# A roll along the columns of an 8192 x 8192 array: which rows of four each DMA queue takes, and how the last 256 rows are cut

## The chip, the cores and the metric

The kernel runs on one core of a Trainium2 chip. A core has sixteen DMA engines, which move data between the chip's memory (HBM) and itself or the core's on-chip memory (SBUF). Transfers are started by instruction queues: here SP (SyncE), ACT (ScalarE) and POOL (GpSimd). The metric is the device time of one execution in microseconds; lower is better.

## The reference

The input is a float32 array of 8192 rows and 8192 columns (32 KB a row, 268 MB in all), and every row is rotated to the right by 100 columns.

```python
def setup_inputs():
    return {"x": np.random.randn(8192, 8192).astype(np.float32), "shift": 100}

def reference(x, shift):
    return np.roll(x, shift, axis=1)
```

Nothing is computed. Each output row is two runs of its input row: columns 100 and up take the input's columns 0 to 8091, and columns 0 to 99 take its last 100.

## The kernel before

The kernel splits the output's columns at `a`. The shift `s` is 100, `a` is 128 rounded up and then raised by 128 to 256, and `g = a - s` is 156. Columns 256 to 8191 (31,744 bytes a row, 97% of the data) go straight from the input in HBM to the output in HBM; columns 0 to 255 go through SBUF.

**The straight copies (lines 34 to 43).** Rows are seen as blocks of 64: block `c`, then `e` from 0 to 15, then `j` from 0 to 3, so row = 64 c + 4 e + j. There are 128 blocks. One DMA of line 43 copies, for one `c` and one `j`, the sixteen rows `e = 0..15`; these rows lie 128 KB apart, and each of the sixteen DMA engines takes one of them. An engine so works on four neighbouring rows in each block, one for each `j`. The queue is `engines[j % 2]`: rows 0 and 2 of the four are issued by SP and rows 1 and 3 by ACT, in the order j = 0, 1, 2, 3. For the last four blocks (256 rows) each copy is cut into two at column `mid` = 4224, two pieces of 3968 columns (15,872 bytes a row), both on the queue of that `j`. This makes 248 whole and 32 / 2 = 16 half copies on each queue.

Each copy signals a semaphore when it has landed on all its engines. The framework hands out eight semaphores for the copies of SP and ACT in turn, and an instruction that takes one up again waits until the copy before it on that semaphore has landed. So at most four copies of each queue are in flight.

**The strip of 256 columns (lines 60 to 82).** The rows are treated in four groups of 2048. For three rows of every four, POOL loads columns -100 to 155 of the row as one run into a tile `t` (line 73; the first 100 of these are the end of the row before). For the fourth row and for the first row's right part it loads the pieces directly into a second tile `h` (lines 74 and 77). DVE then moves the two parts of `t` to the rows of `h` to which they belong (lines 75 and 78), and POOL writes `h` out (line 82). All of POOL's transfers go over a queue of its own and share the sixteen DMA engines with the straight copies. There is no other order between the strip and the copies: they write different columns.

The change touches the loop of lines 37 to 43 alone.

Of the kernel before, what the change touches and what calls it, by code (L numbers as in the profile page):

```python
# [1 line left out]

# [4 lines left out]


@with_exitstack
def kernel(  # L10
    ctx: ExitStack,
    tc: tile.TileContext,
    x: bass.AP,
    shift: int,
    out: bass.AP,
):
    nc = tc.nc
    n_rows, n_cols = x.shape
    s = shift % n_cols
    a = -(-s // 128) * 128  # L20
    if 0 < a <= 384 and a + 128 <= n_cols:
        a += 128
    g = a - s
    P = nc.NUM_PARTITIONS
    engines = [nc.sync, nc.scalar]
    n_chunks = 16
    rows = n_rows // n_chunks

    xm = x.rearrange("(c e j) w -> c j e w", e=16, j=4)
    om = out.rearrange("(c e j) w -> c j e w", e=16, j=4)
    if a < n_cols:
        blocks = n_rows // 64
        mid = (a + n_cols) // 256 * 128
        for c in range(blocks):
            parts = ((a, mid), (mid, n_cols)) if c >= blocks - 4 and a < mid else ((a, n_cols),)  # L40
            for j in range(4):
                for lo, hi in parts:
                    engines[j % 2].dma_start(out=om[c, j, :, lo:hi], in_=xm[c, j, :, lo - s:hi - s])
    if a == 0:
        return


    if a > 512:
        for i in range(n_chunks):
            r = slice(i * rows, (i + 1) * rows)  # L50
            nc.gpsimd.dma_start(out=out[r, :s], in_=x[r, n_cols - s:])
            if g > 0:
                nc.gpsimd.dma_start(out=out[r, s:a], in_=x[r, :g])
        return

    Q, J = 4, 4  # L60
    n_st = n_rows // (P * Q * J)
    reads = ctx.enter_context(tc.tile_pool(name="reads", bufs=n_st))
    heads = ctx.enter_context(tc.tile_pool(name="heads", bufs=n_st))
    xt = x.rearrange("(k p j q) c -> k q p j c", q=Q, j=J, p=P)
    ot = out.rearrange("(k p j q) c -> k q p j c", q=Q, j=J, p=P)
    tiles = []
    for k in range(n_st):
        t = reads.tile([P, Q - 1, J, a], x.dtype)
        h = heads.tile([P, Q, J, a], x.dtype)
        for q in range(1, Q):  # L70
            lead = bass.AP(tensor=x.tensor, offset=(k * P * J * Q + q) * n_cols - s,
                           ap=[[J * Q * n_cols, P], [Q * n_cols, J], [1, a]])
            nc.gpsimd.dma_start(out=t[:, q - 1], in_=lead)  # L73
        nc.gpsimd.dma_start(out=h[:, Q - 1, :, :s], in_=xt[k, Q - 1, :, :, n_cols - s:])  # L74
        nc.vector.tensor_copy(h[:, :Q - 1, :, :s], t[:, :, :, :s])  # L75
        if g > 0:
            nc.gpsimd.dma_start(out=h[:, 0, :, s:], in_=xt[k, 0, :, :, :g])  # L77
            nc.vector.tensor_copy(h[:, 1:, :, s:], t[:, :, :, s:])  # L78
        tiles.append(h)
    for k, h in enumerate(tiles):  # L80
        for q in range(Q):
            nc.gpsimd.dma_start(out=ot[k, q, :, :, :a], in_=h[:, q])  # L82


# [1 line left out]
_INS = ['x', 'shift']  # L86
_OUTS = [((8192, 8192), 'float32')]

_NUMBERS = {'shift': 100}


# [26 lines left out]
```

## Time and profile before

| | |
|---|---|
| median of 5 runs | 828.33 us (825.34 to 829.48) |
| the profiled execution's own time | 825.34 us |
| its span | 823.2 us |
| busy on the core | DVE 7.7 us, POOL 28.8 us |
| DMA packets | 21573, 276.89 MB, mean 336 GB/s |
| issues of line 43 on each of SP and ACT | 248 of 496.0 KB, 16 of 248.0 KB |
| one issue of line 43, median | SP 510 ns, ACT 517 ns |
| last issue of line 43 | SP at 816.8 us, ACT at 817.0 us |

The page is of one execution, taken by the hardware profiler. The DMA digits are the busy share of the sixteen DMA engines in 40 equal slices of the span, in tenths. GB/s counts each byte that a DMA moves once, though a copy from HBM to HBM reads and writes it. A line of the queues gives packets, megabytes and the share of sixteen engines' span that the packets took: q1 and q10 are those of SP and ACT, q0 is that of POOL. A line of the issues gives the destination and source, the queue, how many, the size and the median time from issue to landing. A line of the waits gives who waited for what: total, times, longest. The DMA engines aren't told apart by any view.

### The profile page before, as it was taken

The numbers are of one execution on the slowest core, as the hardware profiler recorded it, in microseconds if no ns is written. First come the engines' busy times: TensorE is split into PE (matmuls) and PEld (weight loads), VectorE is DVE, ScalarE is ACT, GpSimd is POOL, SyncE is SP. The second block draws the span as 40 slices with busy tenths as digits, with TensorE's granted clock in tenths as the row PEclk, the third lists the DMA queues.
The fourth block names the chain that finished last, engine by engine and source line by source line (L and its number), as shares of the span: only waits on it lengthen the run. The fifth ranks groups of instructions, "written<-read, shape, count | busy, mean of one in ns | idle before, by whom it ended". The sixth has DMA issues, their size and how long they took to land. (4 is left out here: it accounts for less than half of the span.)

```text
span 823.2 us, 633 instructions
## 1 busy us (share of the span) xinstructions
DVE 7.7 (1%) x8; POOL 28.8 (4%) x40
## 2 busy tenths in 40 slices
DVE  0000000000000000000000000000000000000000
POOL 3000000000010000000000000000000000000000
DMA  9999999999999999999999999999999999999998
GB/s 302 333 350 344 338 348 344 343 351 344 347 347 367 351 347 349 351 345 352 335 345 333 335 327 326 333 335 326 330 332 326 334 326 324 336 332 322 338 319 290
DMA packets 21573, 276.89 MB, mean 336 GB/s; under 512 B 9025, under 2 KB 9025, under 8 KB 13121
## 3 DMA queue, kind: packets, MB, share of 16 engines
q10 hardware_dynamic: 8448, 130.04, 46.2%
q1 hardware_dynamic: 8448, 130.04, 46.0%
q0 software_dynamic: 4672, 16.78, 7.2%
q14 instruction: 5, 0.03, 0.0%
HBM read 268.44 MB, written 268.44 MB: 652 GB/s over the span
## 5 line engine op out<-in xcount | busy, mean ns | idle before, releaser
L82 POOL DMA_DIRECT2D out_dram<-h x16 | 13.2, 825 | 199.2 <-DMA out_dram<-h 112.8
L73 POOL DMA_DIRECT2D t<-in_x_dram x12 | 9.5, 793 | 60.6 <-DMA t<-in_x_dram 30.3
L75 DVE COPY h<-t 128x1200 f32<-128x1200 f32 x4 | 3.1, 785 | 234.4 <-DMA t<-in_x_dram 234.4
L78 DVE COPY h<-t 128x1872 f32<-128x1872 f32 x4 | 4.9, 1225 | 0.0
L74 POOL DMA_DIRECT2D h<-in_x_dram x4 | 3.0, 748 | 45.7 <-DMA t<-in_x_dram 45.7
L77 POOL DMA_DIRECT2D h<-in_x_dram x4 | 3.0, 749 | 42.6 <-DMA t<-in_x_dram 42.6
L99 POOL MEMSET const-float32-0.0<- 128x1 f32 x1 | 0.1, 98 | 0.2 <-issue 0.2
L99 POOL MEMSET const-bfloat16-1.0<- 128x1 bf16 x1 | 0.1, 101 | 0.0
L99 POOL MEMSET const-float32-1.0<- 128x1 f32 x1 | 0.1, 98 | 0.0
L99 POOL MEMSET const-uint8-127<- 128x1 uint8 x1 | 0.1, 98 | 0.0
## 6 DMA issues: line engine op xcount, KB each, us to landing
out_dram<-in_x_dram ACTq DMA_DIRECT2D x248, 496.0 KB, 12.7
out_dram<-in_x_dram SPq DMA_DIRECT2D x248, 496.0 KB, 12.7
out_dram<-h POOLq DMA_DIRECT2D x16, 512.0 KB, 114.4
t<-in_x_dram POOLq DMA_DIRECT2D x12, 512.0 KB, 95.0
out_dram<-in_x_dram SPq DMA_DIRECT2D x16, 248.0 KB, 6.1
out_dram<-in_x_dram ACTq DMA_DIRECT2D x16, 248.0 KB, 6.1
h<-in_x_dram POOLq DMA_DIRECT2D x4, 312.0 KB, 93.3
h<-in_x_dram POOLq DMA_DIRECT2D x4, 200.0 KB, 98.0
```

Source lines behind the costliest of these rows:

```text
L73: nc.gpsimd.dma_start(out=t[:, q - 1], in_=lead)
L74: nc.gpsimd.dma_start(out=h[:, Q - 1, :, :s], in_=xt[k, Q - 1, :, :, n_cols - s:])
L75: nc.vector.tensor_copy(h[:, :Q - 1, :, :s], t[:, :, :, :s])
L77: nc.gpsimd.dma_start(out=h[:, 0, :, s:], in_=xt[k, 0, :, :, :g])
L78: nc.vector.tensor_copy(h[:, 1:, :, s:], t[:, :, :, s:])
L82: nc.gpsimd.dma_start(out=ot[k, q, :, :, :a], in_=h[:, q])
L99: nc = _bacc.Bacc("TRN2", target_bir_lowering=False, num_devices=1)
```

## The change

The queue of a copy becomes `engines[j // 2]`: rows 0 and 1 of each engine's four are issued by SP and rows 2 and 3 by ACT. The loop runs over j = 0, 2, 1, 3, so that the issues still go to SP and ACT in turn. The cut at `mid` is taken out: the last 256 rows are copied in whole pieces like all the others, 256 copies on each queue.

```diff
     if a < n_cols:
         blocks = n_rows // 64
-        mid = (a + n_cols) // 256 * 128
         for c in range(blocks):
-            parts = ((a, mid), (mid, n_cols)) if c >= blocks - 4 and a < mid else ((a, n_cols),)
-            for j in range(4):
-                for lo, hi in parts:
-                    engines[j % 2].dma_start(out=om[c, j, :, lo:hi], in_=xm[c, j, :, lo - s:hi - s])
+            for j in (0, 2, 1, 3):
+                engines[j // 2].dma_start(out=om[c, j, :, a:], in_=xm[c, j, :, a - s:n_cols - s])
```

## The prediction

> **What bounds the kernel now.** I read the page first, then the DMA issues, then the busy time by stretches, then the waits of SP, and last the packet records. On the page the compute engines hardly appear (DVE 1%, POOL 4%), and the DMA engines are busy from one end to the other.
>
> ```profile
> span 823.2 us, 633 instructions
> DMA  9999999999999999999999999999999999999998
> q10 hardware_dynamic: 8448, 130.04, 46.2%
> q1 hardware_dynamic: 8448, 130.04, 46.0%
> q0 software_dynamic: 4672, 16.78, 7.2%
> HBM read 268.44 MB, written 268.44 MB: 652 GB/s over the span
> out_dram<-in_x_dram ACTq DMA_DIRECT2D x248, 496.0 KB, 12.7
> out_dram<-in_x_dram SPq DMA_DIRECT2D x248, 496.0 KB, 12.7
> out_dram<-in_x_dram SPq DMA_DIRECT2D x16, 248.0 KB, 6.1
> out_dram<-in_x_dram ACTq DMA_DIRECT2D x16, 248.0 KB, 6.1
> ```
>
> The three data queues fill 99.4% of sixteen DMA engines' span, and 92.2% belongs to the copies of line 43. So the time is the bytes over the rate at which they move, and SP, ACT and POOL only feed it. What lies beside the copies (the strips of 256 columns, on POOL and DVE) ends before 380 us and is no part of the end.
>
> The waits of SP show that the queue is held back by landings, not by issue:
>
> ```profile
> SPq L43 <- DMA out_dram<-in_x_dram: 677.1, 259, 4.1
> SPq L113 <- DMA out_dram<-in_x_dram: 4.6, 4, 1.5
> ```
>
> 259 of SP's 264 issues wait for an earlier copy; an issue itself takes 0.51 us (median of its group), 0.51 x 264 = 135 us beside 677 us of waiting. Eight copies are in flight, four on each queue: 8 x 0.508 MB at 327 GB/s is 12.4 us, which is the landing time above.
>
> The stretches, in the columns time, length, DVE, POOL, clock, DMA share, GB/s, show what the halves of the last 256 rows do:
>
> ```profile
> 740.00:760.00 20.00, 0.00 (x0) 0.00 (x0) 1.00 1.00 327
> 790.00:800.00 10.00, 0.00 (x0) 0.00 (x0) 1.00 0.93 317
> 800.00:810.00 10.00, 0.00 (x0) 0.00 (x0) 1.00 0.97 330
> 810.00:820.00 10.00, 0.00 (x0) 0.00 (x0) 1.00 0.99 324
> 818.00:819.00 1.00, 0.00 (x0) 0.00 (x0) 1.00 1.14 333
> 819.00:820.00 1.00, 0.00 (x0) 0.00 (x0) 1.00 0.88 270
> 820.00:821.00 1.00, 0.00 (x0) 0.00 (x0) 1.00 0.78 286
> 821.00:822.00 1.00, 0.00 (x0) 0.00 (x0) 1.00 0.01 0
> ```
>
> The halves start at about 794 us. In their stretch the rate stays about where it was (330 and 324 beside 327), and it holds until the last two microseconds: the engines stop nearly together.
>
> No view prints the single packets, so I worked these from the packet records (start, length, queue). A row of 31,744 bytes is one packet; on one DMA engine packets follow one another within some 10 ns, so from 385 us on, when only SP and ACT copy, the records chain into 16 lines. Three things come out. First, every line alternates SP, ACT, SP, ACT, so before the change an engine copies its four rows as 0, 1, 2, 3, and after it as 0, 2, 1, 3. Second, a row takes 1.174 us at its shortest, and 1.52 us on average after 400 us: a quarter is waiting for memory. Third, the engines aren't level. Over twelve readings, every 20 us from 550 to 770 us, the foremost was 2.9 to 5.3 rows ahead of the hindmost; it can't get much further, because a copy must land on all engines before the fourth next one of its queue is issued.
>
> **The change part by part.** Costs are made against the profiled execution: span 823.2 us, its own time 825.34 us, so 2.1 us lie around the span. That run is the lowest of the five; their median, 828.33, is 3.0 us above it. I add the same microseconds to the median.
>
> Issues: 32 halves become 16 whole copies, 16 issues fewer (8 on each queue). 8 x 0.51 = 4 us of SP, and 8 x 0.52 of ACT; the waits of SP (677 us) cover them, so 0. Without that cover it would be a gain of 4 us at most. The order j = 0, 2, 1, 3 with engine j // 2 still issues SP, ACT, SP, ACT, so the eight semaphores go round as they did, no wait is added, and nothing new is queued behind one. POOL's queue isn't touched.
>
> A rule speaks against my forecast here. The row first: halves take 6.1 us to land beside 12.7 for wholes, and their stretch moves 324 to 330 GB/s beside 327, so smaller copies cost no rate here. The Trainium skill, page "DMA: Bandwidth & Descriptors", section "Bandwidth", advises copies of 1 MiB and more, and its section on the anatomy of one DMA gives a fixed 2.0 us for each on POOL's path. By it, an estimate from that page, 16 copies fewer with eight in flight would save 16 x 2.0 / 8 = 4 us. The trace shows nothing of the kind for SP and ACT, and the sum goes without it.
>
> The end: this is the term that I take. With halves, the eight copies in flight are four rows of an engine instead of eight, so the leading engines are held and the others catch up: the sixteen last packets end between 820.7 and 821.7 us, on average 0.46 us before the last one. With wholes the lead of mid-run reaches the end. A typical reading (about 590 us): the foremost 4.9 rows before the hindmost, and the mean engine 1.9 rows behind the foremost. When the foremost is done, 16 x 1.9 = 30 rows are left. All engines together move 327 GB/s / 31,744 B = 10.3 rows per us, so spread evenly that is 2.9 us. But the hindmost has 4.9 rows to itself. While many engines work, each moves 10.3 / n rows per us; below 12 engines the shortest packet limits it (1 / 1.174 = 0.85 rows per us). Stepped through with that reading's sixteen positions, it takes 5.9 us: 3.0 us lost. Over the twelve readings the loss is 1.5 to 3.5 us, mean 2.75. If the late rows keep taking 1.5 us, it is 2.2 to 5.0, mean 4.0. The late halves of before took between 0.59 and 1.75 us, neither floor nor steady, so I take the middle, 3.4, and subtract the 0.46 that before loses already: **+2.9 us**, with ends +1.0 and +4.6.
>
> The row order: 0, 2, 1, 3 takes away the three steps in four that go on to the next row in memory. By lines and places in a line, rows 0 took 1501 ns, rows 1 1533, rows 2 1512, rows 3 1547 (each +-9). Row 0 comes after a jump of 61 rows and row 2 after its neighbour, both on SP, and row 0 is not longer: -12 +-13 ns. The jump costs nothing that can be seen, and I take **0**. For the ends: two errors each way are -38 to +14 ns for a step, and three quarters of 512 rows change their step, so -15 to +5 us. The other bound is how much the place in memory alone moves the rate: the stretches of 100 us from 400 to 800 us carried 335, 329, 331 and 328 GB/s with the same issue, +1.4% and -0.8% about their mean of 331, which over the 814 us up to the end is -11 to +7 us. This bounds gain and loss alike, and I keep -12 to +8.
>
> Sum: 0 + 2.9 + 0. The profiled execution would go from 825.34 to 828.2; the median from 828.33 to **831.2 us**, 0.35% slower. A measurement of this kernel can tell about 0.3% (2.5 us) from no change.
>
> **The rivals.**
>
> *The memory likes the new order (faster).* The mechanism: the packets' wait above 1.174 us is for memory, and rows two apart may meet fewer busy places of it than neighbours do. It takes place in all 512 rows of an engine. Against it: sixteen engines stand on rows spread over several of the four places anyway (up to five rows apart), so the order within a group reshuffles who meets whom but changes little on average; and the rows' means differ by the queue (SP 1506, ACT 1540) rather than by the step. For it: a row waits 0.35 us, so there is something to win. It decides from 2.9 us / 512 = 5.7 ns a row, 0.4% of 1.52 us; to be faster by 0.3% it needs 10.5 ns. Price at 1%: -8 + 2.9 = -5, so 823 us; at the bound 819.
>
> *The memory dislikes it (clearly slower).* Same place, opposite sign: a row that goes on where the last one ended finds its memory ready, and a jump doesn't. Against it stand the -12 +-13 ns. For it: the order before read and wrote 128 KB runs straight through, and the packet that pays needn't be the one I charged. At 0.8%: +7 + 2.9, so 838 us.
>
> *Nothing is seen.* The lead shrinks by itself: at the last two readings, 750 and 770 us, it was 3.2 and 2.9 rows, still on whole copies. Then the loss is 1.5 to 1.8 us by the floor, less 0.46: +1.2, so 829.5 us. That the change doesn't do what it says I exclude: wholes and rows are written into the issues.
>
> **How the numbers follow.** Forecast, the end costs its 1.0 to 4.6 us and the order less than 0.3%: 0.38, of which about 0.27 lies over the 2.5 us and 0.11 within. Slower by the order: 0.22. Nothing seen: 0.13. Faster by the order: 0.27. So slower 0.27 + 0.22 = 0.49, same 0.11 + 0.13 = 0.24, faster 0.27. The forecast's own range is 829.3 to 832.9. The whole range has to reach into the cases of the order: below, to 821, which leaves out the part of a gain beyond some 1.2%; above, to 841, which leaves out a loss beyond that bound.
>
> **What would show it.** Right: 256 issues on each of SP and ACT, all of 496 KB; about 327 GB/s until some 6 us before the last packet, then falling for 5 us or so, to a few engines at work (DMA share below 0.5 for two microseconds); the last packets' ends spread over 4 us or more instead of 1.0; mid-run stretches from 400 to 780 us within 1% of those of before. Wrong in the end term: the share stays above 0.8 until a microsecond before the last packet. Wrong in the order term: the stretches between 400 and 780 us move by over 1% against before, all in one direction, with the mean row away from 1.52 us; then the rate and not the end tells the time.

## The result, and the profile after

Over 39 runs the changed kernel takes 829.84 us (median), over 68 runs the kernel before takes 828.02. The ratio is 1.0021 with a 95% interval of 1.0014 to 1.0028: 1.7 us slower, between 1.2 and 2.3. The forecast was slower by 2.9 us, 831.2 us, with 829.3 to 832.9 as its own range.

The page after, with the same lines as before:

```profile
span 828.1 us, 617 instructions
DMA  9999999999999999999999999999999999999997
q1 hardware_dynamic: 8192, 130.04, 46.5%
q10 hardware_dynamic: 8192, 130.04, 45.7%
q0 software_dynamic: 4672, 16.78, 6.7%
HBM read 268.44 MB, written 268.44 MB: 648 GB/s over the span
out_dram<-in_x_dram ACTq DMA_DIRECT2D x256, 496.0 KB, 12.8
out_dram<-in_x_dram SPq DMA_DIRECT2D x256, 496.0 KB, 12.8
```

The halves are gone, and a whole copy lands as it did. The waits of SP (its copies are on line 40 now) show the same queue, held back by landings, but the last line, the wait for the last copies, has grown from 4.6 us:

```profile
SPq L40 <- DMA out_dram<-in_x_dram: 680.8, 252, 4.0
SPq L110 <- DMA out_dram<-in_x_dram: 10.2, 4, 2.9
```

Mid-run before, in the columns time, length, DVE, POOL, clock, DMA share, GB/s:

```profile
400.00:500.00 100.00, 0.00 (x0) 0.00 (x0) 1.00 1.00 335
500.00:600.00 100.00, 0.00 (x0) 0.00 (x0) 1.00 0.99 329
600.00:700.00 100.00, 0.00 (x0) 0.00 (x0) 1.00 1.00 331
700.00:800.00 100.00, 0.00 (x0) 0.00 (x0) 1.00 0.99 328
```

The stretches after, in the same columns:

```profile
400.00:500.00 100.00, 0.00 (x0) 0.00 (x0) 1.00 0.99 332
500.00:600.00 100.00, 0.00 (x0) 0.00 (x0) 1.00 0.99 328
600.00:700.00 100.00, 0.00 (x0) 0.00 (x0) 1.00 1.00 327
700.00:800.00 100.00, 0.00 (x0) 0.00 (x0) 1.00 0.99 329
810.00:820.00 10.00, 0.00 (x0) 0.00 (x0) 1.00 0.98 327
821.00:822.00 1.00, 0.00 (x0) 0.00 (x0) 1.00 0.38 159
822.00:823.00 1.00, 0.00 (x0) 0.00 (x0) 1.00 0.23 95
823.00:824.00 1.00, 0.00 (x0) 0.00 (x0) 1.00 0.22 95
824.00:825.00 1.00, 0.00 (x0) 0.00 (x0) 1.00 0.30 127
825.00:826.00 1.00, 0.00 (x0) 0.00 (x0) 1.00 0.15 63
```

Two things are to be seen. Mid-run the rate is that of before within 1.2% (332, 328, 327, 329 against 335, 329, 331, 328). And the end is no longer sharp: from 822 us on, some four engines of sixteen are at work, a share of about 0.25, at some 95 GB/s. The packet records (one line of packets for each engine) say the same: twelve lines end between 821.5 and 822.7 us, four between 825.8 and 826.6. All ten rows that start after 822.6 us take 1.174 or 1.175 us each, the shortest time of a row in the profile before (1.174 us); the mean row after 400 us takes 1.53 us. The mean line ends 3.52 us before the last one; before it was 0.46 us. I call this the **end loss**, and take it from the packet records of each run.

This profiled execution took 830.25 us, 4.9 above that of before. 3.1 us of it is end loss (3.52 - 0.46); the rest is of the size by which executions of one kernel differ (before: 824.1 to 831.0).

### The profile page after: what moved, and what is told of

Same layout as the page of the kernel before. It is cut to its first block, busy times and chain, and to the rows that moved or that the text cites. A ratio compares the mean times of both kernels' runs of the same rounds, so it can differ in the third digit from the quotient of the medians.

```text
span 828.1 us, 617 instructions
## 1 busy us (share of the span) xinstructions
DVE 7.7 (1%) x8; POOL 28.8 (3%) x40
```

## The experiments

The theory: the change costs what the engines' lead costs at the end (the wholes). The rival: the rows' order on an engine changes the rate. Differences from the kernel before are of the means of the runs on the same chip, with 95% intervals.

**The order alone, halves kept.**

```diff
-            for j in range(4):
+            for j in (0, 2, 1, 3):
                 for lo, hi in parts:
-                    engines[j % 2].dma_start(out=om[c, j, :, lo:hi], in_=xm[c, j, :, lo - s:hi - s])
+                    engines[j // 2].dma_start(out=om[c, j, :, lo:hi], in_=xm[c, j, :, lo - s:hi - s])
```

> The new row order (SP rows 0 and 1, ACT rows 2 and 3, j = 0, 2, 1, 3) with the last 256 rows still in halves. End theory: the sixteen last packets end within about 1 us, mean loss at the end about 0.5 us, time as before, 828.0 +-0.8 us (ratio 0.999 to 1.001). Order theory (the 1.8 us come from the rows' order): 829.8 us, ratio 1.002, with the row's mean packet longer by some 3 ns over the whole run and the end as tight as before.

830.75 us against 830.23, ratio 1.001 (0.9997 to 1.0023); difference +0.4 +-0.8 us. The end loss is 0.87 us, and the engines are at work nearly to the last microsecond:

```profile
824.00:825.00 1.00, 0.00 (x0) 0.00 (x0) 1.00 1.20 381
825.00:826.00 1.00, 0.00 (x0) 0.00 (x0) 1.00 0.83 302
826.00:827.00 1.00, 0.00 (x0) 0.00 (x0) 1.00 0.26 95
```

The time lies nearer to the end theory's number, but its interval reaches the rival's.

**The wholes alone, old order.**

```diff
-        mid = (a + n_cols) // 256 * 128
         for c in range(blocks):
-            parts = ((a, mid), (mid, n_cols)) if c >= blocks - 4 and a < mid else ((a, n_cols),)
             for j in range(4):
-                for lo, hi in parts:
-                    engines[j % 2].dma_start(out=om[c, j, :, lo:hi], in_=xm[c, j, :, lo - s:hi - s])
+                engines[j % 2].dma_start(out=om[c, j, :, a:], in_=xm[c, j, :, a - s:n_cols - s])
```

> The old row order, the last 256 rows in whole pieces. End theory: the sixteen last packets end over 3 to 5 us, three or four engines last, mean loss 2 to 3.5 us at the end, time 829.8 to 831 us, ratio 1.002 to 1.0035. Order theory: 828.0 us, ratio 1.000.

831.71 us against 830.23, ratio 1.001 (0.9995 to 1.0025); difference +1.15 +-0.9 us. The end loss is 2.91 us and the last packets end over 4.9 us. Its stretches:

```profile
821.00:822.00 1.00, 0.00 (x0) 0.00 (x0) 1.00 1.03 381
822.00:823.00 1.00, 0.00 (x0) 0.00 (x0) 1.00 0.38 159
823.00:824.00 1.00, 0.00 (x0) 0.00 (x0) 1.00 0.44 190
824.00:825.00 1.00, 0.00 (x0) 0.00 (x0) 1.00 0.45 191
825.00:826.00 1.00, 0.00 (x0) 0.00 (x0) 1.00 0.37 159
400.00:800.00 400.00, 0.00 (x0) 0.00 (x0) 1.00 1.00 328
```

So the wholes alone bring back the slack end, with six late engines here. The times of these two runs don't yet separate the theories, so both were run again beside the whole change.

**Both parts again, and the whole change, on one chip.**

> The new row order with halves at the end, once more, beside the two kernels below on one chip. The first time it stood at 1.001 (0.9997 to 1.0023). End theory: 0 to 0.6 us over the kernel before, last packets ending within 1 to 2.4 us. Order theory: 1.7 us over it, with the end as tight.

> The old row order with wholes at the end, once more. End theory, now with its refund (the halves of before pay some 0.4 us at the change to halves and 0.5 us at the end, wholes pay 2.5 to 3.5 us at the end): 1.3 to 2.5 us over the kernel before, last packets ending over 4 to 6 us. Order theory: 0 to 0.5 us over it.

> The changed kernel beside the two halves of the change. If the parts add up, its time over the kernel before is the sum of theirs, about 1.8 us (1.2 to 2.3 from the many runs of the result), most of it from the wholes.

| | time, against 827.7 | ratio (95%) | difference of means | end loss |
|---|---|---|---|---|
| order alone | 828.56 | 1.0016 (1.0000 to 1.0032) | +0.9 +-1.1 | 0.77 |
| wholes alone | 829.40 | 1.0021 (1.0010 to 1.0031) | +1.5 +-0.75 | 3.36 |
| both | 830.62 | 1.0040 (1.0025 to 1.0055) | +2.8 +-0.9 | 3.22 |

With the earlier runs, each weighted by the inverse square of its interval: order +0.6 +-0.6 us, wholes +1.35 +-0.6, both (39 and 6 runs) +2.0 +-0.4. The parts add up to 1.95. The wholes cost something clear of the noise, so the rival cannot be the whole cause: it would have put some 1.8 us on the order and nothing on the wholes. Whether the order costs anything beside them stays open between 0 and 1.2 us. The rates from 400 to 800 us show no effect of the order: 329, 329, 329 and 331 GB/s in the four profiles with the new order (after, the order alone twice, the whole change again), 331, 328 and 329 in the three with the old one (before, the wholes alone twice).

**A coarser end.** The old order and whole pieces, but the last 1024 rows in copies of two neighbouring rows for each engine (`xm2` and `om2` are the same views with the two rows kept beside each other):

```diff
+            if c >= blocks - 16:
+                for j in (0, 2):
+                    engines[j // 2].dma_start(out=om2[c, :, j:j + 2, a:], in_=xm2[c, :, j:j + 2, a - s:n_cols - s])
+                continue
```

> Old order up to the last 1024 rows; there one copy takes two neighbouring rows of each engine (SP rows 0 and 1, ACT rows 2 and 3), so eight copies in flight are sixteen rows of an engine instead of eight. End theory: the engines' lead may grow beyond the present 5 to 10 rows in the last 1024 rows; if it reaches 12 rows the hindmost ends 6 to 9 us after the rest and the mean loss is 5 to 8 us, so 833 to 836 us; if it doesn't grow in that short a stretch, 830 to 831 us as with plain wholes. Rival (the rate and not the end tells the time): 828 us, since the rate in the stretch of mid-run is the same.

833.10 us against 830.23, ratio 1.0033 (1.0015 to 1.0050), difference of the means +2.4 +-1.1 us. The expectation counted from 828 us; from this chip's own 830.23 it is the end theory's number for a lead that doesn't grow (2 to 3 us), and it is against the rival's (0). The last packets end over 7.4 us (819.5 to 826.9), end loss 4.0 us, with 330 GB/s from 400 to 800 us. Larger pieces at the end cost more at the end, and nothing is seen to be lost before it.

**Halves everywhere.**

```diff
-            parts = ((a, mid), (mid, n_cols)) if c >= blocks - 4 and a < mid else ((a, n_cols),)
+            parts = ((a, mid), (mid, n_cols))
```

> Old order, halves for all 8192 rows instead of the last 256. If halves cost no rate, as the rows of the last 256 suggest, 828 us (ratio 0.998 to 1.002), with a lead of the engines of 2 to 4 rows all through and the same tight end. If each copy has a fixed cost that eight in flight don't hide (some 6 us to land against a receipt of 1 to 2 us), engines idle by several per cent: at 3% of idle that memory doesn't make good, 850 us. The page's fixed 2.0 us for each copy, spread over eight in flight, would make 496 more copies cost 124 us.

832.23 us against 830.23, ratio 1.0026 (1.0009 to 1.0043), difference of the means +2.1 +-1.2 us. The end loss is 0.47 us, as expected, but the time is not that of before. These stretches, and then those of before:

```profile
0.00:400.00 400.00, 7.70 (x8) 28.83 (x40) 1.00 1.00 342
400.00:800.00 400.00, 0.00 (x0) 0.00 (x0) 1.00 1.00 327
```

```profile
0.00:400.00 400.00, 7.70 (x8) 28.84 (x40) 1.00 1.00 345
400.00:800.00 400.00, 0.00 (x0) 0.00 (x0) 1.00 1.00 331
```

The rate is lower all through. The two profiles overstate by how much: the profiled execution of before (825.34 us) is 2.7 us below the median of its kernel, the one here (832.29) at its own. By the times, 496 copies more cost about 2 us, some 4 ns each. Whether that is a slower rate of busy engines or short idle times is not settled: 0.01 of the share in 400 us is 4 us. Halves are not free, but for the 256 rows of before (16 copies more) this is below 0.1 us. The fixed 2.0 us for a copy on POOL's path (Trainium skill, page "DMA: Bandwidth & Descriptors", section "Anatomy of one DMA"), weighed in the prediction, does not carry over to SP and ACT here. By an estimate from that page, 496 copies more with eight in flight would have cost 124 us.

**Two rows a copy, everywhere; and the same with halves in the last 512 rows.** The first issues as in the coarser end above, for all blocks; the second does so for all but the last eight blocks, which go in halves in the new order.

> All straight copies take two neighbouring rows of each engine (SP rows 0 and 1, ACT rows 2 and 3), 1 MB a copy, to the very end: eight copies in flight are sixteen rows of an engine. End theory: the engines' lead grows towards 10 to 16 rows, and the hindmost engines end 7 to 12 us after the foremost; mean loss at the end 5 to 8 us, so 833 to 838 us beside some 830 for the kernel before on this chip. Rival (the end doesn't count because the rate makes it good, or fewer and larger copies are better): 826 to 830 us.

> The same two-row copies, but the last 512 rows in halves of one row, which hold the lead down to four rows. End theory: the last packets end within 1 to 2 us, and the time is 4 to 7 us below that of the two-row copies up to the end, 829 to 831 us. Rival (the end doesn't count): the two agree within 1 us, although their last packets end over 10 us in one and over 1 us in the other.

838.12 us against 828.29, ratio 1.0105 (1.0075 to 1.0135), and 836.23, ratio 1.009 (1.0068 to 1.0113). The first goes the way the end theory said, and a little further: 9.8 us above this chip's own 828.29, where 3 to 8 had been expected above 830. The second does not: it was to be at 829 to 831 us. It was also to be 4 to 7 us below the first and is 1.7 +-3.4 us below (difference of the means), an interval too wide to tell 4 us from none. The stretches show why it is so slow. Two rows everywhere, at its end:

```profile
822.00:824.00 2.00, 0.00 (x0) 0.00 (x0) 1.00 0.93 349
824.00:826.00 2.00, 0.00 (x0) 0.00 (x0) 1.00 0.33 143
826.00:828.00 2.00, 0.00 (x0) 0.00 (x0) 1.00 0.15 63
830.00:832.00 2.00, 0.00 (x0) 0.00 (x0) 1.00 0.07 32
834.00:836.00 2.00, 0.00 (x0) 0.00 (x0) 1.00 0.07 32
```

One engine works alone for the last 6.6 us; the end loss is 10.4 us. With halves in the last 512 rows, where the copies change:

```profile
760.00:770.00 10.00, 0.00 (x0) 0.00 (x0) 1.00 1.02 337
770.00:780.00 10.00, 0.00 (x0) 0.00 (x0) 1.00 0.61 210
780.00:790.00 10.00, 0.00 (x0) 0.00 (x0) 1.00 0.66 219
790.00:800.00 10.00, 0.00 (x0) 0.00 (x0) 1.00 0.96 341
820.00:830.00 10.00, 0.00 (x0) 0.00 (x0) 1.00 0.92 310
```

Its last packets end within 1.2 us. But for 20 us the engines that had run ahead stand still until the hindmost has caught up: (330 - 210 + 330 - 219) x 10 / 330 = 7 us are lost there. In this profile the halves did not remove the cost of the lead. They moved it from the end to the place where the pieces become smaller.

**Other places in memory.** Once with the sixteen rows of a copy side by side, 32 KB apart:

```diff
-    xm = x.rearrange("(c e j) w -> c j e w", e=16, j=4)
+    xm = x.rearrange("(c j e) w -> c j e w", e=16, j=4)
```

> The kernel before with another place in memory for the engines: in a block an engine takes the rows e, 16 + e, 32 + e and 48 + e, so the sixteen rows of a copy lie side by side (32 KB apart instead of 128 KB) and an engine's next row is 512 KB further. It tells how much the order of rows in memory can move the rate at all. If the rate depends little on it, 829 to 832 us, the mean packet 1.52 us within 1%. If neighbours on one engine matter (no step goes on to the next row any more), 835 us or more, with a longer packet all through. A gain, by less meeting of the engines in memory: 825 us or below.

835.39 us against 828.29, ratio 1.009 (1.0077 to 1.0103), with an end nearly as tight as before (1.5 us from first to last line). From 400 to 800 us:

```profile
400.00:800.00 400.00, 0.00 (x0) 0.00 (x0) 1.00 1.00 325
```

The rate falls by 1.8% against the 331 of the one profile before and by 1.2% against the 329 of the order alone, the mean packet from 400 to 800 us rises from 1.52 to 1.55 us. So the place of the rows in memory does move the rate, when the distance of the engines' rows and the step of an engine both change.

Once with eight neighbouring rows for an engine, 256 KB apart:

```diff
-    xm = x.rearrange("(c e j) w -> c j e w", e=16, j=4)
+    xm = x.rearrange("(c e j) w -> c j e w", e=16, j=8)
-        blocks = n_rows // 64
+        blocks = n_rows // 128
-            parts = ((a, mid), (mid, n_cols)) if c >= blocks - 4 and a < mid else ((a, n_cols),)
+            parts = ((a, mid), (mid, n_cols)) if c >= blocks - 2 and a < mid else ((a, n_cols),)
-            for j in range(4):
+            for j in range(8):
```

`om` changes as `xm` does, here and in the edit above.

> The kernel before with blocks of 128 rows: an engine takes eight neighbouring rows, and the sixteen rows of a copy are 256 KB apart instead of 128 KB. With rows side by side (32 KB apart, a step of 512 KB on an engine) the rate fell by 0.9%. If long straight runs on one engine are what the memory likes, eight rows are the same or better, 0.997 to 1.000; if the distance between the engines' rows is what counts, it could go either way by 0.5 to 1%; the last packets end within 1 to 2 us as before.

832.57 us against 827.70, ratio 1.0053 (1.0035 to 1.0072), difference of the means +3.9 +-1.5 us. The end loss is 0.43 us, but part of the time is lost at the change to halves: in the packet records the 8 us from 800 to 808 us carry 266 GB/s, which is 1.6 us against 330. Longer straight runs on an engine do not help, so they are not what the kernel before lives on; the distance between the engines' rows may be, but the run does not separate it from the order in which queues and rows now meet. None of the twelve runs was faster than the kernel before.

**Marks on the engines.** The changed kernel, but its last 64 rows are cut by columns: 3840 columns in copies of 16 rows, 2048 in copies of 8, 1280 in copies of 4 and 768 in copies of 2.

```diff
+        cuts = ((16, a, a + 3840), (8, a + 3840, a + 5888), (4, a + 5888, a + 7168), (2, a + 7168, n_cols))
+        for k, lo, hi in cuts:
+            for i in range(64 // k):
+                r = slice(top + i * k, top + (i + 1) * k)
+                engines[i % 2].dma_start(out=out[r, lo:hi], in_=x[r, lo - s:hi - s])
```

> The changed kernel with its last 64 rows cut otherwise, to mark the engines by the sizes of their last packets: 15,360 bytes of each row in copies of sixteen rows, 8192 bytes in copies of eight rows, 5120 in copies of four, 3072 in copies of two. A copy of n rows uses n engines, so the lines of packets fall into classes that can be told apart. If the engines that hang back belong to one group (the first eight, or the other eight), the hindmost lines of mid-run fall into one class; if it changes from run to run, they are spread over the classes. The end itself is slow here, since the last copies use few engines: 835 to 850 us, which says nothing on the change.

846.07 us in its one run. The last whole rows of twelve lines end between 815.3 and 816.5 us, those of the other four at 817.7, 818.0, 818.4 and 820.0. Each of these four goes on with four packets of the sixteen-row mark, which end at 820.04, 820.35, 820.72 and 822.26 us, and 8 or 9 ns after each of these ends a packet of the eight-row mark starts. The other twelve lines have all ended the first mark by 819.31 us, and the first eight-row copy starts on only four of them, between 819.54 and 819.62 us. Four early lines and the four late ones make the eight that an eight-row copy uses. So in this run all four hindmost engines are among these eight, and none is among the other eight. Whether that is so in every run, one run can't tell; which of the smaller marks they carry is not as clear.

## Why the prediction was right, and where it was off

*What bounds.* Held: the rate of the copies from one end to the other.

*Issues at 0.* Held: 252 waits of SP for 256 copies, none new. That smaller copies cost no rate held for the 256 rows of before (below 0.1 us), not as a rule: in all rows they cost 2.1 +-1.2 us.

*The order at 0, with -12 and +8.* The value lies at the lower edge of what was measured (+0.6 +-0.6 us), the ends were far too wide. Of the four mid-run stretches one moved by more than the 1% that was set (331 to 327, 1.2%), and not all moved in one direction; the mean row took 1.53 us. (The bound of +1.4% was read too high: 335 is 1.2% over the mean of 331. Nothing rests on the difference.) My worry that memory dislikes a jump was not borne out at the size of that rival. The favoured rows of the one profile before did not return either: after 400 us SP's rows took 1506 ns and ACT's 1542 there, in the profile after SP's took 1551 and ACT's 1508. That a row waits for memory was my name for the time above 1.174 us. The late rows at 1.175 us show that the wait is gone when few engines are at work; what it is for, no run tells.

*The end at +2.9.* The mechanism was right, the size was not: the wholes alone cost 1.35 +-0.6 us. The term had two parts. The loss of the wholes, 3.4 us, held: 3.52, 2.91, 3.36 and 3.22 us in the four profiles with whole pieces, mean 3.25. But it held by luck in part. I took the middle between late rows at their shortest (mean 2.75 us) and late rows at 1.5 us (4.0 us). The late rows run at their shortest, 1.175 us each, so by my own stepping the loss should have been 2.75. The measured 3.25 is above that mean of the twelve readings, though inside their range (1.5 to 3.5 us).

What was too small is what before already loses, 0.46 us. The three profiles with halves in the last 256 rows lose 0.46, 0.87 and 0.77 us at the end, mean 0.7. And they can pay at the change to halves, where I booked nothing: the leading engines are held back there until the others catch up. I read "324 to 330 beside 327" from stretches of 10 us, in which a short dip is hidden. Sharing each packet's bytes over its time, 8 us behind the change carry 316 GB/s in the profile of before (804 to 812 us), 313 with the order alone (800 to 808) and 294 in its second run (796 to 804). Against 330 this is 0.3, 0.4 and 0.9 us, mean 0.5. Only the third stands clear: between 560 and 780 us, where nothing changes, single stretches of 8 us go down to 314, 309 and 319 GB/s in these three profiles.

So what the profiles show puts the step at 3.25 - 0.7 = 2.55 us, or at 2.05 with the mean of 0.5 for the change to halves. The measured cost of the wholes, 1.35 +-0.6 us, ends at 1.95, a little below both. Where the rest went stays open. That a change of piece size collects the lead is shown on the large scale by the two-row kernel with halves (7 us) and by the eight-row kernel (1.6 us); for the 256 rows of before it is seen in one dip of three.

*The sum.* The end was put too high by some 1.5 us, the order perhaps too low by some 0.6. The two misses go opposite ways, so the total came out nearer than its largest term.

*Rivals.* In number "Nothing is seen" came closer than the forecast: its 1.2 us and the forecast's 2.9 stand on the two sides of 1.7. It was wrong in its cause, a lead that shrinks by itself: the end was as slack as forecast, and a part of the difference is that the halves were dearer than I thought.

*What would show it.* Share below 0.5 for five microseconds, last packets over 5.1 us, 327 GB/s until then: as written. Only the one mid-run stretch at 1.2% lies outside what was set.

## What to carry to other kernels

Where transfers fill the DMA engines to the end, look at how level the engines finish: up to the number of pieces in flight, some engines run ahead, and the others finish alone, here at the shortest time that a row takes (1.175 us). Smaller pieces at the end shrink that, but a large lead is then paid where the pieces become smaller; count both places, in stretches no longer than a few pieces and beside stretches of the same length in which nothing changes, before booking the gain. And don't pay for the tight end in the whole run: halves everywhere made the end as level and the kernel 2 us slower.

## What the hardware showed that I had not expected

The sixteen engines are far from level in a copy that gives each exactly the same bytes. Four to six of them ended 3 to 5 us behind the rest in each of the four profiles with whole pieces, and with two rows a copy one engine was 6.6 us behind all others. In the one run with marks, the four hindmost were all among the eight engines that an eight-row copy uses. The rate of the copy depends on where its rows lie: 325 GB/s with the sixteen rows of a copy 32 KB apart and 512 KB to an engine's next row, against 329 to 331 with 128 KB and 32 KB (835.39 against 828.29 us); which of the two distances counts, and why, no run here tells.
